# A two-layer hybrid encoder on one core: groups of the feed-forward part of 3, 4, 5, 5, 5 chunks instead of 4, 5, 5, 5, 3, and some weight lows by adding transfers

## The chip, the cores and the metric

The kernel runs on one core of a Trainium2 chip. The metric is the device time of one execution in microseconds (us). Engines are named as in the profile: PE (TensorE, matmul), PEld (its weight loads), DVE (VectorE), ACT (ScalarE), POOL (GpSimd), SP (SyncE, which issues the weight transfers). Each engine works through its own queue in the order in which the program was written; semaphores tie the queues together.

## The reference

Two layers over x of 512 tokens and 1024 features in float32. Each layer: an RMS norm; latents, queries, keys and values for two attentions, channels for a pooling branch, and gates; an attention with latent projections (MLA, 8 heads) and one with grouped queries (GQA, 8 heads on 2 key heads); the three branches projected, gated, summed, projected and added to x; then the feed-forward part, which this case is mostly about:

```python
D_MODEL, SEQ, DEPTH, D_FF = 1024, 512, 2, 2816

hf = rms_norm(x, ffn_norm_g[l])
u = depthwise_conv(hf @ ffn_w_up[l], ffn_conv_w[l], ffn_conv_b[l])   # width 3, along the tokens
u_gate, u_val = u[..., :D_FF], u[..., D_FF:]
x = x + (jax.nn.silu(u_gate) * u_val) @ ffn_w_down[l]
```

## The kernel before

**Numbers in two halves.** Features lie on the 128 partitions and the 512 tokens along the rows. Each float32 operand is split into a high half, rounded to the matmul's format, and a low half, the rest; a product is three matmuls, high by high, high by low, low by high (`mm3`). For activations the halves are `HH`, `HL` (the normed x) and `act` or `ah`, `al` (the gated product); for weights `wh`, `wl`, and `fh`, `fl` where a weight tile serves as an operand of its own.

**Weights.** SP's queue brings raw weight tiles in the order of use, into three wide tiles (`RAW`) and eight single ones (`ALONE`); a raw tile that comes free issues the next transfer. A unit of weights (128 x 512 or narrower) is split some units ahead of its use. The high is a copy on ACT. The low is made in one of two ways: a unit of kind "p" by a subtraction on DVE or POOL, whichever the planner thinks sooner; a unit of kind "u" by `by_transfer`: ACT writes the negative of the high, and a transfer that POOL issues adds the raw tile to it in memory.

```python
    def by_transfer(hi, lo, r):
        A.activation(hi, r, AF.Copy)
        A.activation(lo, f(hi), AF.Copy, scale=-1.0)
        ...
        nc.gpsimd.dma_start(f(lo), r, accum_op=ALU.add)
```

**What sets the order.** The program is written out by a planner while it records: a clock advances with each matmul, steps that depend on each other wait in chains (`chain`), and each is emitted to its engine's queue when the planner's estimate says that its time has come; `need` emits everything that an operand still lacks. The planner's costs only decide order; on the chip the engines wait for each other by semaphores.

**The stages of a layer.** Latents, pooling and GQA projections (0 to 82 us in the first layer); the two attentions, with projections, gates and branch outputs as fillers between their matmuls (to 355); the last of them and the output projection (to 427); the feed-forward part (to 772). The second layer does the same. In the attention, the scores' maxima use one PSUM bank, `ps_S`: a score matmul `ps_S<-ka,qa` writes it, a reduction `nm<-ps_S` on DVE reads it and frees it for the next. The "n" units are the key weights of the MLA attention, two units of 256 columns per layer.

**The feed-forward part.** The 2816 hidden features are 22 chunks of 128, each with a gate and a value part, in groups of `SIZES`. The first group is *plain*: each part is 24 matmuls of 512 columns (8 blocks of features by 3). The other chunks are *products*: four blocks of a 2 x 2 scheme are computed with seven half-size products instead of eight (`FORMS`, 84 matmuls of 256 columns per chunk), with sums of weight tiles (`s`, `raw<-raw,s`) and of activations (`tf`) as operands. Copies of banks between the products are the rows `sx<-ps_..` on ACT (`aside`): product "3" needs the copy that is made after product "2". The norm's factor `rbc` is applied when a bank is read; for the first plain parts `norm_finish` makes it: a small matmul `ps_S<-prt,C`, POOL's power, DVE's rows.

**The down-projection.** Each finished chunk gives `act`. Its *tokens* (g, m, i), three matmuls for output row m and chunk i of group g, are dealt into the products of the next group at four `SPOTS`; of the last but one group, two rows (`KEEP`) are kept for the end, where they are followed by the last group's own tokens. Output rows alternate between the banks mi and S; each is added to `XM` by DVE, which frees the bank. Places for `act` are kept by `keep_act`: six fixed ones for some chunks, slots of the common pool for others.

Of the kernel before, what the change touches and what calls it, by code (L numbers as in the profile page):

```python
# [41 lines left out]
PRE_A = 16  # L42
PRE_B = 8
LA, LAP, LAF = 3, 4, 6
SIZES = (4, 5, 5, 5, 3)
PLACE = (0, 4, 0, 5, 0)
ROOM = 6
KEEP = 2
FORMS = ("11", "12", "1", "22", "2", "4", "3")
SPOTS = ("22", "2", "4", "3")  # L50
# [4 lines left out]
        "mla": (-6.2, -2.9, -1.0, 0.1, 0.64, 1.678, 1.82, 35.5)}  # L55

D_ROW, D_OUT, D_IN, D_LAT = 3.4, 3.2, 4.0, 6.0
D_SUM, D_FIRST = 2.0, 2.4
D_ISSUE, D_ADD = 0.9, 4.5
REST = 0.4  # L60
W_BIAS = 2.54
# [14 lines left out]
def _order(br):  # L76

    r, lag = [], LAG[br]  # L80
    for m in range(KC + lag):
        r += [(k, pos.index(m)) for k, b, pos in EXTRA if b == br and m in pos]
        if m < KC:
            r.append(("g", m))
        if m >= lag:
            r.append(("b", m - lag))
    return r
# [6 lines left out]
def _widths():  # L94

    r = [384] * KC + [T] * 8 + [T] * KC + [288] * MID + [T] + [288] * (KC - MID)
    r = [("p", wd) for wd in r]
    for br in (2, 1, 0):
        late = []
        for k, m in _order(br):  # L100
            added = k in "gb" and br == 0 or br == 1 and (k == "v" or k == "g" and 1 <= m <= 3)
            ws = [("u" if added else "p", wd) for wd in WIDTHS[k]]
            if k in "nv":
                late = ws
            else:
                r += ws[:1] + late + ws[1:]
                late = []
    return r + [("u", T)] * (2 * KC)


def _groups():
    e = np.cumsum(SIZES)
    return [(int(b - n), int(b)) for n, b in zip(SIZES, e)]


def _ffn():
# [4 lines left out]
    for g, (c0, c1) in enumerate(_groups()):  # L121
        dealt = len(late) - (KEEP * SIZES[g - 1] if g == len(SIZES) - 1 else 0)
        for n, c in enumerate(range(c0, c1)):
# [14 lines left out]
def _layer_units():  # L138

    r = _widths()  # L140
    for tok in _ffn():
        if tok[0] == "u":
            r += [("u", T), ("p", T), ("next",)]
        elif tok[0] == "f":
            r.append(tok)
        elif (tok[2] * SIZES[tok[1]] + tok[3]) % 4 == 0:
            r.append(("u" if tok[1] < len(SIZES) - 1 else "p", T))
    return r


def _stream():


    pieces, slots, units, alone = [], [], [], []
    early, plain, fresh = [], 0, False
    for kind, *u in _layer_units() * L:
        if kind == "next":
            plain = (plain + 1) % (2 * SIZES[0])
            if plain and plain >= 2 * SIZES[0] - 8:
                early.append(len(slots))  # L160
                slots.append(T)
                alone.append(True)
            continue
        if kind == "f":
            if u[1] == FORMS[0]:
                first, fresh = len(pieces), True
                for _ in range(4):
                    if early:
                        pieces.append((early.pop(0), 0, T))
                        continue  # L170
                    pieces.append((len(slots), 0, T))
                    slots.append(T)
                    alone.append(True)
            units.append((u[1], first))
            continue
        if len(slots) <= KC or fresh or alone[-1] or slots[-1] + u[0] > 1024:
            slots.append(0)
            alone.append(False)
        fresh = False
        pieces.append((len(slots) - 1, slots[-1], u[0]))  # L180
        slots[-1] += u[0]
        units.append((kind, len(pieces) - 1))
    return pieces, slots, units, alone
# [25 lines left out]
class Clock:  # L209
# [37 lines left out]
    def done(self, *key):  # L247
        self.ready[key] = self.fin + self.SEM

    def need(self, *keys):  # L250
        for k in keys:
            while k not in self.ready:
                self.pop()
            self.to(self.ready[k])
# [4 lines left out]
    def chain(self, *steps, after=0.2):  # L259

        def go(n, source=None):
            if n == len(steps):
                return
            keys, fn = steps[n] if isinstance(steps[n], tuple) else ((), steps[n])
            late = [self.ready.get(k, self.now + 0.5) for k in keys]
            if late and max(late) > self.now:
                self.at(max(late) - self.now, lambda: go(n))
                return
            self.fin, self.source, self.last = self.now, source, None
            fn()  # L270
            source, self.source = self.last, None
            self.at(max(0.0, self.fin - self.now), lambda: go(n + 1, source))
        self.at(after, lambda: go(0))
# [65 lines left out]
def trunk(ctx: ExitStack, tc: tile.TileContext, x, w, prm, gb, cst, out):  # L339
    nc = tc.nc  # L340
    ctx.enter_context(tc.manual_schedule())
    ck = Clock()
# [16 lines left out]
    def slot(name, dt=F32):  # L359
        uid[0] += 1  # L360
        t = sp.tile([P, SLOT], dt, tag="s", name=f"{name}_{uid[0]}")
        return t
# [5 lines left out]
    def small(name, shape, dt=F32, bufs=2):  # L368
        uid[0] += 1
        t = sm.tile(shape, dt, tag=name, name=f"{name}_{uid[0]}", bufs=bufs)  # L370
        return t
# [4 lines left out]
    def ps(tag):  # L376
        while not banks[tag]:
            ck.pop()
        ck.to(heapq.heappop(banks[tag]))
        uid[0] += 1  # L380
        t = pp.tile([P, T], F32, tag=tag, name=f"ps_{tag}_{uid[0]}", bufs=nbank[tag])
        return t
# [8 lines left out]
    def free(tag):  # L391
        heapq.heappush(banks[tag], ck.fin + ck.SEM)
# [3 lines left out]


    pieces, swidth, units, alone = _stream()
    soff = np.concatenate([[0], np.cumsum(swidth)]) * P
    st = {"dma": 0, "split": 0, "use": 0, "ffn": False}  # L400
# [125 lines left out]
    def mm(o, lhsT, rhs, start, stop, again=False):  # L526
        PE.matmul(o, lhsT=lhsT, rhs=rhs, start=start, stop=stop, skip_group_check=again)  # L527
        n = rhs.shape[-1]
        ck.to(ck.now + (n / 2400.0 + 0.0133 if st["ffn"] else max(0.107, n / 2370.0)))
# [86 lines left out]

    def norm_finish(gen, out, force=False):

        if gen not in parts or not (force or ck.ready.get(("prt", gen), 1e9) + (D_FIRST if gen in (0, 1, 3) else D_SUM) <= ck.now):
            return  # L620
        need(("prt", gen))
        s2 = ps("S")
        mm(s2[:, :16], C[:, C_GRP:C_GRP + P], parts.pop(gen), True, True)
        a, a4 = small("fac", [P, 16]), small("fac4", [P, 16])
        rt, rbc = out["rt"], out["rbc"] = small("rt", [P, 4]), slot("rbc")

        def mean():
            V.tensor_scalar(a, s2[:, :16], 1.0 / D, EPS, ALU.mult, ALU.add)
            free("S")

        def tokens():
            V.tensor_tensor(a4, a, C[:, C_SEL:C_SEL + 16], ALU.mult)
            V.tensor_reduce(rt, a4.rearrange("p (b g) -> p b g", g=4), AX.X, ALU.add)
            done("rt", gen)

        def rows():
            V.transpose(rbc[:, :T].rearrange("p (j r) -> p j r", r=32), bc(a.unsqueeze(2), [P, 16, 32]))
            done("rbc", gen)

        chain(mean, lambda: G.tensor_tensor(a, a, bc(mhalf, [P, 16]), ALU.pow), tokens, rows, after=0.3)  # L640
# [13 lines left out]
    parts = {}  # L654

    def bc(ap, shape):
        return ap.to_broadcast(shape)
# [26 lines left out]
    def layer(l, sq, xsrc):  # L684
# [151 lines left out]
        for g in range(4):  # L836
            acc = ps(ptags[g])
            for n, _ in enumerate(feat_major(acc, G1)):
                norm_finish(G1, nrm, g == 1 and n == 7)
            chain(*pool_steps(g, acc, ptags[g]))  # L840
# [37 lines left out]
        for b in range(4):  # L878
            v = slot("vg", F32R)
# [769 lines left out]
        def keep_act(c):  # L1649
            g = next(i for i, (c0, c1) in enumerate(groups) if c0 <= c < c1)  # L1650
            i = c - groups[g][0]
            n = 2 * (PLACE[g] + i)
            if n < 2 * ROOM:
                return places[n], places[n + 1]
            return slot("ah", F32R)[:, :T], slot("al", F32R)[:, :T]

# [220 lines left out]
def _pack_weights(i):  # L1877
    res = []
    for l in range(L):
# [34 lines left out]
        for kind, *tok in _ffn():  # L1914
# [8 lines left out]
            elif kind == "d":  # L1923
                g, m, k = tok
                c0, c1 = _groups()[g]
                if (m * (c1 - c0) + k) % 4 == 0:
                    at = [divmod(m * (c1 - c0) + k + n, c1 - c0) for n in range(4)]
                    res.append(np.concatenate([dn[(c0 + k_) * P:(c0 + k_ + 1) * P, m_ * P:m_ * P + P]
                                               for m_, k_ in at], axis=1))
    pieces, swidth, _, _ = _stream()  # L1930
    assert [a.shape[1] for a in res] == [wd for _, _, wd in pieces]
    slots = [[] for _ in swidth]
# [79 lines left out]
```

## Time and profile before

| | |
|---|---|
| median of 3 runs | 1547.4 us (1546.53 to 1547.94) |
| profiled execution | 1548.79 us, span 1547.0 us |
| granted clock of TensorE | 1.000 |
| busy, share of the span | PE 99%, DVE 76%, ACT 69%, POOL 50% |
| transfers | 241.79 MB, 156 GB/s; queue q1 (SP) 34.3% of 16 engines, q0 (POOL) 29.0% |

The page gives busy times of each engine, the chain of work that ended last, groups of instructions and the time from a transfer's issue to its landing. The views quoted later are: the table by stage (for each stretch its length, and for each engine its busy time and number of instructions, then the granted clock, the transfers' share and GB/s), the waits of one engine (who was waited for, total, times, longest), the chain (start, length, what), and the timeline (start, length, engine, line, operation, output <- inputs, in brackets the idle time before it and who ended that). A matmul's row lasts longer than its share of TensorE, since matmuls are pipelined; the distance of two starts is what one costs.

### The profile page before, as it was taken

The page shows a single profiled execution, that of the slowest core. Times are in us where ns is not written, and L with a number is a line of the kernel's source. Part 1 is how long each engine was busy: PE and PEld are TensorE (multiplying, and loading weights), DVE is VectorE, ACT ScalarE, POOL GpSimd, SP SyncE. Part 2 cuts the span into 40 slices and gives each one's busy share as a digit, 9 for nine tenths or more (in the row PEclk, how much of TensorE's full clock was granted, in tenths as well). Part 3 has the DMA queues.
Part 4 walks back from the last instruction along what each step waited for, and adds up shares of the span by engine and source line. Part 5 has one row for each costly group of instructions (what it writes and reads, how often), then busy time and mean ns, then how long its engine had stood idle before and what let it go on. Part 6 is the DMA issues. An engine that isn't in the chain of part 4 may idle for free.

```text
span 1547.0 us, 24549 instructions
## 1 busy us (share of the span) xinstructions
PE 1537.7 (99%) x8337; PEld 1342.7 (87%) x8337; DVE 1169.6 (76%) x1960; ACT 1073.5 (69%) x2010; POOL 768.6 (50%) x826
## 2 busy tenths in 40 slices
PE   9999999999999999999999999999999999999998
PEld 8888888888889999999898888888888898999997
DVE  6877886776688888888656678768666888888884
ACT  5557875877677877777544587758766687777772
POOL 3984886753452323232488648766535422222222
PEclk9999999999999999999999999999999999999999
DMA  5432354658978788877534323546599778788763
GB/s 204 124 118 83 87 125 140 161 130 204 216 181 203 179 185 188 193 177 150 138 117 136 118 76 86 134 139 174 116 223 212 198 182 178 179 191 189 176 134 109
DMA packets 139517, 241.79 MB, mean 156 GB/s; under 512 B 30976, under 2 KB 53504, under 8 KB 139392
## 3 DMA queue, kind: packets, MB, share of 16 engines
q1 hardware_dynamic: 91872, 162.93, 34.3%
q0 software_dynamic: 42624, 77.09, 29.0%
q8 instruction: 65, 1.06, 0.3%
q10 hardware_dynamic: 4896, 0.21, 0.2%
q14 instruction: 60, 0.49, 0.1%
HBM read 149.41 MB, written 13.63 MB: 105 GB/s over the span
## 4 chain that ended last, share of the span: by engine, by line
PE 88%; issue 4%; DMA 3%; DVE 2%; POOL 2%; ACT 1%; SPq 0%; ACTq 0%; POOLq 0%; DVEq 0%
PE ps_acc L527 40%; PE ps_AV L527 16%; PE ps_ST L527 15%; PE ps_S L527 9%; PE ps_mi L527 8%; DMA raw<-w 1%; POOL wl L307 1%; DMA fl<-raw 1%; POOL win L307 0%; DMA wl<-raw 0%; DVE a L311 0%; ACT wh L300 0%; DMA qb<-nm 0%; DVE ctl L311 0%; DVE u L307 0%
## 5 line engine op out<-in xcount | busy, mean ns | idle before, releaser
L439 POOL DMA_DIRECT2D wl<-raw x188 | 168.9, 903 | 386.0 <-ACT wl L300 184.7
L300 ACT ACTIVATE wh<-raw 128x512 fp32r<-128x512 f32 (+2 forms) x449 | 265.1, 605 | 66.3 <-DVE raw L307 16.4
L307 POOL TENSOR_TENSOR wl<-raw,wh 128x512 fp32r<-128x512 f32 (+3 forms) x167 | 213.5, 1287 | 169.0 <-ACT wh L300 150.8
L439 POOL DMA_DIRECT2D fl<-raw x108 | 94.4, 874 | 168.6 <-ACT fl L300 62.7
L527 PE MATMUL ps_acc<-HH,wh 128*128 128x512 f32 x400 | 156.8, 392 | 0.4 <-DVE XM L311 0.4
L527 PE MATMUL ps_acc<-HH,wl 128*128 128x512 f32 x400 | 156.6, 391 | 0.1
L527 PE MATMUL ps_acc<-HL,wh 128*128 128x512 f32 x400 | 156.5, 391 | 0.0
L311 DVE SCALAR_TENSOR_TENSOR a<-u,prm,a 128x511 f32<-128x511 f32 x176 | 133.7, 762 | 22.8 <-ACT a L300 22.3
L300 ACT ACTIVATE wl<-wh 128x512 fp32r<-128x512 f32 (+1 forms) x188 | 118.1, 628 | 5.9
L315 DVE TENSOR_REDUCE nm<-ps_S 128x1 fp32r<-128x512 f32 x128 | 87.9, 687 | 44.8 <-PE ps_S L527 43.8
L300 ACT ACTIVATE a<-u,prm 128x512 f32<-128x512 f32 x88 | 71.2, 811 | 53.1 <-DVE u L307 52.9
L527 PE MATMUL ps_acc<-tf,wh 128*128 128x256 f32 x576 | 106.2, 282 | 0.0
L527 PEld LDWEIGHTS ps_acc<-tf,wh 128*128 128x128 f32 x576 | 94.3, 191 | 6.0
L527 PEld LDWEIGHTS ps_acc<-HH,wl 128*128 128x128 f32 x400 | 75.1, 188 | 16.7 <-DMA wl<-raw 0.5
L527 PEld LDWEIGHTS ps_acc<-HH,wh 128*128 128x128 f32 x400 | 75.4, 188 | 15.4 <-issue 0.7
L527 PEld LDWEIGHTS ps_acc<-HL,wh 128*128 128x128 f32 x400 | 75.3, 188 | 15.4
L307 DVE TENSOR_TENSOR wl<-raw,wh 128x512 fp32r<-128x512 f32 (+2 forms) x95 | 69.1, 728 | 20.0 <-ACT wh L300 19.5
L527 PE MATMUL ps_acc<-tf,wl 128*128 128x256 f32 x288 | 81.5, 283 | 0.0
L527 PE MATMUL ps_AV<-HH,wl 128*128 128x256 f32 (+1 forms) x240 | 78.2, 326 | 0.0
L527 PE MATMUL ps_AV<-HL,wh 128*128 128x256 f32 (+1 forms) x240 | 78.2, 326 | 0.0
L527 PE MATMUL ps_AV<-HH,wh 128*128 128x256 f32 (+1 forms) x240 | 78.2, 326 | 0.0
L300 ACT ACTIVATE fl<-fh 128x512 fp32r<-128x512 f32 x108 | 68.4, 633 | 3.4
(426 smaller groups left out, 5029.8 us busy)
## 6 DMA issues: line engine op xcount, KB each, us to landing
raw<-w SPq DMA_DIRECT2D x153, 512.0 KB, 4.0
wl<-raw POOLq DMA_DIRECT2D x184, 256.0 KB, 4.1
raw<-w SPq DMA_DIRECT2D x151, 256.0 KB, 3.7
fl<-raw POOLq DMA_DIRECT2D x108, 256.0 KB, 5.0
raw<-w SPq DMA_DIRECT2D x13, 384.0 KB, 3.1
XM<-x SPq DMA_DIRECT2D x16, 256.0 KB, 4.4
dtq<-tr SPq DMA_DIRECT2D x16, 192.0 KB, 2.0
dtk<-tr SPq DMA_DIRECT2D x16, 192.0 KB, 3.1
```

The costliest lines, as they stand in the source:

```text
L300: return self.eng.activation(out, in_, func, **k)
L307: return self.eng.tensor_tensor(out, *a)
L311: return self.eng.scalar_tensor_tensor(out, *a)
L315: return self.eng.tensor_reduce(out, in_, *a, **k)
L439: nc.gpsimd.dma_start(f(lo), r, accum_op=ALU.add)
L527: PE.matmul(o, lhsT=lhsT, rhs=rhs, start=start, stop=stop, skip_group_check=again)
```

## The change

- `SIZES` goes from 4, 5, 5, 5, 3 to 3, 4, 5, 5, 5: three plain chunks in place of four, and five chunks in the last group in place of three.
- `PLACE` names the places of `act` for each group: the first three chunks of every group get a fixed place, alternately 0 to 2 and 3 to 5, the others slots. `ROOM` is gone.
- The two "n" units of each layer become "u" units, whose lows are made by adding transfers.
- `_stream` gives early raw slots for single tiles after all six plain parts; before it did so after seven of eight.
- `D_FIRST` has one entry for each norm. Only the first differs: 3.2 in place of 2.4, the time after `prt` at which the planner emits the first norm's small matmul.

```diff
-SIZES = (4, 5, 5, 5, 3)
-PLACE = (0, 4, 0, 5, 0)
-ROOM = 6
+SIZES = (3, 4, 5, 5, 5)
+PLACE = ((0, 1, 2), (3, 4, 5), (0, 1, 2), (3, 4, 5), (0, 1, 2))
...
-D_SUM, D_FIRST = 2.0, 2.4
+D_SUM, D_FIRST = 2.0, (3.2, 2.4, 2.0, 2.4)
...
-            added = k in "gb" and br == 0 or br == 1 and (k == "v" or k == "g" and 1 <= m <= 3)
+            added = k in "gb" and br == 0 or br == 2 and k == "n" or br == 1 and (k == "v" or k == "g" and 1 <= m <= 3)
...
-            if plain and plain >= 2 * SIZES[0] - 8:
+            if plain >= 2 * SIZES[0] - 8 or not plain:
...
-        if gen not in parts or not (force or ck.ready.get(("prt", gen), 1e9) + (D_FIRST if gen in (0, 1, 3) else D_SUM) <= ck.now):
+        if gen not in parts or not (force or ck.ready.get(("prt", gen), 1e9) + D_FIRST[gen] <= ck.now):
...
-            n = 2 * (PLACE[g] + i)
-            if n < 2 * ROOM:
+            if i < len(PLACE[g]):
+                n = 2 * PLACE[g][i]
                 return places[n], places[n + 1]
```

The planner then writes another order in the attention and in the feed-forward part. Three places of it follow; names are the program's, and a number at a name's end only tells tiles apart.

DVE's queue in the first layer's attention (about 155 to 163 us of the profile), before:

```order
L311 SCALAR_TENSOR_TENSOR vt_1702<-ps_mi_1759,vg_73_587,vt_1702 128x512
L307 TENSOR_TENSOR wl_1817<-raw_1554,wh_1816 128x512
L327 RECIPROCAL oinv_1777<-otr_1776 128x16
L307 TENSOR_TENSOR wl_1845<-raw_1593,wh_1844 128x256
L307 TENSOR_TENSOR pl_1815<-ps_ST_1811,ph_1814 128x512
L315 TENSOR_REDUCE ssm_1028<-mns_1829 128x8
L315 TENSOR_REDUCE nm_1873<-ps_S_1874 128x1
L307 TENSOR_TENSOR gt_1885<-ps_acc_1793,rbc_404 128x512
L315 TENSOR_REDUCE ssm_1028<-mns_1864 128x8
L315 TENSOR_REDUCE nm_1873<-ps_S_1886 128x1
```

And of the changed program, from the same `vt` row:

```order
L310 SCALAR_TENSOR_TENSOR vt_1719<-ps_mi_1769,vg_73_581,vt_1719 128x512
L330 STREAM_TRANSPOSE otr_1789<-osum_1637 128x512
L326 RECIPROCAL oinv_1790<-otr_1789 128x16
L314 TENSOR_REDUCE ssm_1028<-mns_1825 128x8
L322 COPY MK_157<-ps_acc_1855 128x8x64
L306 TENSOR_TENSOR pl_1846<-ps_ST_1841,ph_1845 128x512
L306 TENSOR_TENSOR wl_1879<-raw_1598,wh_1878 128x512
L306 TENSOR_TENSOR gt_1876<-ps_acc_1791,rbc_409 128x512
L314 TENSOR_REDUCE ssm_1028<-mns_1863 128x8
L314 TENSOR_REDUCE nm_1894<-ps_S_1895 128x1
L310 SCALAR_TENSOR_TENSOR XM<-gt_1702,ps_acc_1877 128x512
```

Both weight lows (`wl`) ahead of the reduction `nm` are gone from DVE; a later unit's low stands there instead. POOL's queue in the changed program has them, the 256-wide one as a transfer (DMA) behind two subtractions:

```order
L306 TENSOR_TENSOR MQ_155<-MQ_155,ssm_1028 128x768
L306 TENSOR_TENSOR wl_1793<-raw_1559,wh_1792 128x512
L306 TENSOR_TENSOR MQ_155<-MQ_155,ssm_1028 128x768
L306 TENSOR_TENSOR wl_1810<-raw_1559,wh_1809 128x512
L438 DMA wl_1814<-raw_1598 128x256
```

ACT's queue at the first product chunk of the first layer (about 473 to 478 us), before, from the last plain part's convolution to the high of its `act`:

```order
L300 ACTIVATE a_5135<-u_5134,prm_91 128x512
L300 ACTIVATE sx_5138<-ps_acc_5140 128x256
L300 ACTIVATE wh_5161<-s_802_5112 128x512
L300 ACTIVATE wh_5186<-raw_4968 128x512
L300 ACTIVATE wl_5187<-wh_5186 128x512
L300 ACTIVATE fh_5208<-raw_4708 128x512
L300 ACTIVATE fl_5209<-fh_5208 128x512
L300 ACTIVATE sx_5139<-ps_AV_5185 128x256
L300 ACTIVATE act_4718<-a_5135 128x512
```

And after:

```order
L299 ACTIVATE a_5046<-u_5045,prm_91 128x512
L299 ACTIVATE wh_5072<-s_796_5023 128x512
L299 ACTIVATE wh_5095<-raw_4865 128x512
L299 ACTIVATE wl_5096<-wh_5095 128x512
L299 ACTIVATE fh_5120<-raw_4710 128x512
L299 ACTIVATE fl_5121<-fh_5120 128x512
L299 ACTIVATE sx_5050<-ps_AV_5094 128x256
L299 ACTIVATE fh_5140<-raw_4797 128x512
L299 ACTIVATE fl_5141<-fh_5140 128x512
L299 ACTIVATE sx_5050<-ps_ST_5119 128x256
L299 ACTIVATE act_4719<-a_5046 128x512
```

The pair `fh`, `fl` of the next weight tile and one more `sx` now stand ahead of the high of the last plain chunk's `act`.

ACT's queue in the last product chunk of the first layer (about 743 to 748 us), before; `sx_8480` is the copy that product "3" needs:

```order
L300 ACTIVATE sx_8481<-ps_ST_8543 128x256
L300 ACTIVATE wh_8577<-raw_8398 128x512
L300 ACTIVATE wl_8578<-wh_8577 128x512
L300 ACTIVATE sx_8480<-ps_acc_8482 128x256
L300 ACTIVATE wh_8607<-raw_8398 128x512
L300 ACTIVATE wh_8611<-raw_8584 128x512
L300 ACTIVATE a_8628<-u_8478,prm_91 128x512
```

And after, where it is `sx_8500`:

```order
L299 ACTIVATE sx_8501<-ps_ST_8561 128x256
L299 ACTIVATE wh_8587<-raw_8271 128x512
L299 ACTIVATE wl_8588<-wh_8587 128x512
L299 ACTIVATE wh_8592<-raw_8404 128x512
L299 ACTIVATE ah_8486<-a_8485 128x512
L299 ACTIVATE sx_8500<-ps_acc_8502 128x256
L299 ACTIVATE wh_8619<-raw_8404 128x512
L299 ACTIVATE wh_8645<-raw_8629 128x512
```

A weight copy (`wh_8592`) and the high of the chunk before (`ah_8486`) have come between.

## The prediction

> **What bounds the kernel now.** The page comes first: TensorE is busy for all but 9.3 us of the span, and 88% of the chain that ended last is matmul.
>
> ```profile
> span 1547.0 us, 24549 instructions
> PE 1537.7 (99%) x8337; PEld 1342.7 (87%) x8337; DVE 1169.6 (76%) x1960; ACT 1073.5 (69%) x2010; POOL 768.6 (50%) x826
> PE 88%; issue 4%; DMA 3%; DVE 2%; POOL 2%; ACT 1%; SPq 0%; ACTq 0%; POOLq 0%; DVEq 0%
> ```
>
> So time goes in two ways only: the matmuls that must be issued, and the few places where TensorE stands. The chain gives a matmul's price: 24 of 512 columns take 5.44 us (0.2267 each), 12 of 256 columns take 1.44 (0.120 each).
>
> ```profile
> 388.53 5.44 PE ps_ST L527 x24
> 473.70 1.44 PE ps_AV L527 x12
> ```
>
> The table by stage says where TensorE stands: almost nothing in the first layer's feed-forward part (355 to 704), but 0.75 us at its end, and 1.64 in one place of the second layer's.
>
> ```profile
> 355.00:470.00 115.00, 114.88 (x507) 94.47 (x507) 82.05 (x124) 77.25 (x137) 52.47 (x50) 1.00 0.89 212
> 470.00:704.00 234.00, 234.00 (x1641) 219.51 (x1640) 196.01 (x333) 179.35 (x334) 64.16 (x74) 1.00 0.82 184
> 704.00:760.00 56.00, 55.25 (x343) 49.54 (x342) 39.66 (x64) 35.49 (x66) 18.51 (x19) 1.00 0.60 130
> 1243.00:1300.00 57.00, 55.36 (x393) 51.95 (x392) 46.59 (x80) 43.34 (x82) 16.50 (x19) 1.00 0.85 191
> ```
>
> TensorE's own waits name them: one weight low that an adding transfer brought late, two waits for a PSUM bank at the end of a feed-forward part, two in the attention, one at the start.
>
> ```profile
> PE ps_ST L527 <- DMA fl<-raw: 1.6, 1, 1.6
> PE ps_S L527 <- DVE XM L307: 1.5, 2, 0.8
> PE ps_S L527 <- DVE nm L315: 0.6, 2, 0.3
> PE ps_S L527 <- DVE prt L315: 0.3, 1, 0.3
> ```
>
> All terms below are changes of the profiled execution, 1548.8 us (span 1547.0 and 1.8 around it); the median of the runs is 1547.4, and I carry the same difference over to it.
>
> **The matmul work: −1.5, certain.** In each layer one chunk goes from plain to seven half-size products. Plain it is 48 matmuls of 512 columns, 48 × 0.2267 = 10.88 us; as products 84 of 256, 84 × 0.120 = 10.08. That is −0.80 a layer, −1.60 in all. The last row of the output is done in halves over the last group, which grows from three chunks to five: its extra work is 12 more matmuls of 256 for 6 of 512, +0.08. Sum −1.52.
>
> **The lows of the "n" units by transfer: −1.7.** At 156 to 162 VectorE makes two weight lows itself and stands 1.29 us for ScalarE's high of the second. Behind it in the same queue are the reductions that free the score bank, S:
>
> ```profile
> 156.15 0.85 DVE L307 TENSOR_TENSOR wl<-raw,wh 128x512 fp32r<-128x512 f32 x1 [0.22 <-ACT wh L300]
> 158.45 1.53 DVE L307 TENSOR_TENSOR wl<-raw,wh 128x256 fp32r<-128x256 f32 x1 [1.29 <-ACT wh L300]
> 161.10 0.67 DVE L315 TENSOR_REDUCE nm<-ps_S 128x1 fp32r<-128x512 f32 x1
> 159.75 0.62 PE L527 MATMUL ps_S<-ka,qa 128*128 128x512 f32 x1
> 160.22 0.39 PE L527 MATMUL ps_AV<-ph,vg 128*128 128x512 f32 x1
> 161.14 0.40 PE L527 MATMUL ps_acc<-HH,wl 128*128 128x512 f32 x1
> 161.83 0.62 PE L527 MATMUL ps_S<-ka,qa 128*128 128x512 f32 x1 [0.29 <-DVE nm L315]
> 162.29 0.40 PE L527 MATMUL ps_ST<-qa,ka 128*128 128x512 f32 x1
> ```
>
> The starts of these matmuls should be 0.23 apart; they are 0.47, 0.69 and 0.46, so TensorE loses 0.24 + 0.46 + 0.23 = 0.93 a layer. In the new order both rows are gone from VectorE there: the 512-wide low is GpSimd's and the 256-wide one a transfer, and the two score matmuls stand further apart. I take 0.85 a layer. What speaks against it: the new transfer is issued only 7.3 us of matmuls before its use and stands behind two GpSimd subtractions. If those hold it for 2 us and it takes the page's median for such lows (4.1 us, below), 1.2 us are left. If it takes 8.12, as the slowest one quoted below, TensorE waits 2.8. Range −2.3 to +1.
>
> ```profile
> wl<-raw POOLq DMA_DIRECT2D x184, 256.0 KB, 4.1
> fl<-raw POOLq DMA_DIRECT2D x108, 256.0 KB, 5.0
> ```
>
> The Trainium skill ("SBUF — State Buffer", section "SBUF: two separate sides") has a rule against this edit: a transfer issued from GpSimd's queue waits while VectorE holds the ports the two share. By it the new low could be one VectorE row (0.7 us) later; 0.5 of the 1.2 would be left, and the sum stays. No row here shows such a wait by itself.
>
> **The start: −0.1.** The new first entry of `D_FIRST` puts the mean's matmul three matmuls later, which takes away the 0.3 wait for `prt` above. Its result is then 0.2 later for the chain of GpSimd steps that TensorE waits for at 76. Between −0.5 and +0.3.
>
> **The plain stage: −0.4.** Here transfers are the limit (share 0.89). One low landed 0.05 before its matmul, and 0.4 us of gaps lie around it:
>
> ```profile
> 453.89 6.15 DMA wl<-raw
> 460.09 5.30 PE ps_acc L527 x22
> ```
>
> One plain chunk fewer, and slots for the raw tiles of all six plain parts, give this stretch air. 0 to −0.5.
>
> **The first product chunk: +1.2.** What is new is a wait for the last plain chunk's activation. Now the product stage begins at 470.66, the low of that activation is done at 478.94, 8.28 later, and its first reader stands at 481.36:
>
> ```profile
> 470.66 0.28 PE L527 MATMUL ps_acc<-HH,fh 128*128 128x256 f32 x1
> 477.60 0.62 ACT L300 ACTIVATE act<-a 128x512 fp32r<-128x512 f32 x1
> 478.25 0.69 DVE L307 TENSOR_TENSOR act<-a,act 128x512 fp32r<-128x512 f32 x1 [1.00 <-ACT act L300]
> 481.36 0.63 PE L527 MATMUL ps_mi<-act,wh 128*128 128x512 f32 x2
> 443.00:471.00 28.00, 27.88 (x124) 22.71 (x123) 23.88 (x35) 20.30 (x33) 11.76 (x12) 1.00 0.87 211
> ```
>
> So 2.42 us are to spare. With three plain chunks the last one's first token is the third of the group instead of the fourth: the need moves three 512-wide matmuls and two products forward, to 8.56 (high) and 8.79 (low) after the start. The unchanged chain would leave 0.3 to 0.4. But in the new order two copies of feed-forward weights (`fh`, `fl`, 0.62 each) and one `sx` stand ahead of ScalarE's high, and VectorE, busy 24 of 28 us, has a weight low and a raw sum ahead of the scaling. I put the high at 7.9 to 8.6 and the low at 9.35: 0.6 late in each layer. From 0 (VectorE keeps its lead) to 1.5 a layer.
>
> **Short leads of adding transfers: −0.4.** One place costs 1.8 now: the low issued at 1291.05 took 8.12 us and its matmul, due at 1297.41, ran at 1299.21.
>
> ```profile
> 1291.05 8.12 DMA fl<-raw
> 1297.29 0.28 PE L527 MATMUL ps_ST<-HL,fh 128*128 128x256 f32 x1
> 1299.21 0.39 PE L527 MATMUL ps_ST<-HH,fl 128*128 128x256 f32 x1 [1.64 <-DMA fl<-raw]
> ```
>
> In the program this low is issued 6.8 us of matmuls ahead of its use, of which 6.4 were left on the chip. Counting so, the feed-forward part has three lows per layer now under 8 us: 6.8, 7.4 and 7.6. The new order keeps such a chunk (6.8, 7.6, 7.8) and adds thirteen more lows per layer: 7.0, 7.0, 7.3, twice 7.5, 7.5 and 7.6, and in the last group 7.7, 7.7, 7.8 and 8.0. A token of the down-projection is three 512-wide matmuls, 0.68 us, so a chunk with six tokens passes in 10.08 + 6 × 0.68 = 14.2 us; before, only the first product group (6.4 tokens) came near that. One of the six short ones is late now, by 1.8. For the 26 new ones, whose lead is 0.2 to 1.2 longer than that one's, I take half the chance and a third of the lateness: 26 / 12 × 0.6 = 1.3, and 0.1 for the old ones; 1.4 instead of 1.8. Range −1.8 (none late) to +5.
>
> The Trainium skill prices such a transfer at 2.0 us + bytes / 436e3 ("DMA: Bandwidth & Descriptors", section "Anatomy of one DMA — SWDGE (gpsimd) path"): 2.6 us for 256 KB, an estimate from that page. The trace disagrees: 5.0 at the median and 8.12 here. By the page no lead of 6.4 could be short, and this term would be −1.8; as a rival that is weighed below.
>
> **The end of each feed-forward part: −0.3.** TensorE now waits 0.75 for the S bank:
>
> ```profile
> 748.01 0.63 ACT L300 ACTIVATE wh<-raw 128x512 fp32r<-128x512 f32 x1 [2.19 <-PE ps_acc L527]
> 749.38 2.88 DVE L311 SCALAR_TENSOR_TENSOR a<-u,prm,a 128x511 f32<-128x511 f32 x2 [2.85 <-ACT a L300]
> 753.57 0.68 DVE L307 TENSOR_TENSOR XM<-ps_S,XM 128x512 f32<-128x512 f32 x1
> 754.31 0.74 PE L527 MATMUL ps_S<-act,wh 128*128 128x512 f32 x2 [0.75 <-DVE XM L307]
> 744.87 0.37 ACT L300 ACTIVATE sx<-ps_acc 128x256 f32<-128x256 f32 x1
> 746.50 0.40 PE L527 MATMUL ps_acc<-tf,wh 128*128 128x256 f32 x2
> ```
>
> ScalarE's weight copy held the convolution's first step, and VectorE's row that frees S stood behind the rest. With five chunks in the last group the bank is needed 0.6 us of matmuls later after more rows, and this stall (0.75 busy, 0.9 by starts) about goes: −1.0 a layer. But the last product ("3") needs the copy `sx` of the bank that product "2" wrote. Now that copy ends 1.27 before product "3". In the new order it stands behind a weight copy that waits for product "4" (2.8 after "2") and one more: 2.8 + 0.63 + 0.62 + 0.37 = 4.4 against 3.5 of matmuls, +0.85 a layer. Net −0.15 a layer, between −1.0 and +0.3.
>
> **Sum.** −1.5 −1.7 −0.1 −0.4 +1.2 −0.4 −0.3 = −3.2: 1545.6 for the profiled execution, 1544.2 for the median. That is just over what a measurement of this kernel can tell from no change, 0.2% or 3.1 us.
>
> **Rivals.**
> - *The waits eat the gain.* The activation is 1.5 us late in each layer (+3.0 for +1.2), and the score bank's wait only moves (−0.8 for −1.7): −0.5, 1546.9. For it: VectorE's 24 of 28 us. Against: the wait names the same bank in both layers, and its cause is gone from the queue.
> - *Slower: the six-token cadence makes lows late.* If a low in each of the five chunks with the shortest leads of a layer takes 8.1 as at 1291, they come 1.7, 1.5 and three times 1.0 late: 6.2 a layer, 12.4 in all in place of 1.8. With the other terms (−2.8) that is +7.8, 1555.2. It decides from 0.8 us a chunk on, ten chunks. For it: that one low, in the only group of such a cadence. Against: the same place of the first layer shows no wait, and one of 108 is late.
> - *Transfers and activation in time.* No low is late (−1.8), VectorE keeps its lead (0 for +1.2): −5.8, 1541.6. The page's rule above would give its first half.
>
> **How the numbers follow.** The forecast has 0.50; its own terms move it between −5 and −1, and a little over half of that lies beyond the bound: 0.29 faster, 0.21 same. Transfers and activation in time: 0.17, faster. The waits eat the gain: 0.21, same. Slower by late lows: 0.12. So faster 0.46, same 0.42, slower 0.12. The range, 1540.5 to 1549.0, takes in the first two rivals and small lateness, and leaves out the slow one and part of the best.
>
> **What would show it.** TensorE's busy time falls by about 1.5 to 2. VectorE's low of 256 columns is gone near 158, and the S score matmul there starts without a gap. At the third token of the first product group TensorE shows a wait for `act`, 0 to 1.5 us, in both layers; product "3" of the last chunk waits for `sx`, and XM's wait for S is gone. I am wrong if `fl` waits add up to more than 4 us, or if the attention's gaps are as long as before.

## The result, and the profile after

The changed kernel takes 1564.95 us (median of 4 runs, 1563.12 to 1566.65) against 1547.18 (median of 4, 1546.53 to 1547.94): 1.0116 times the time before, 95% interval 1.01 to 1.0132. It is 17.8 us slower; 1544.2 was forecast, and the range ended at 1549.0. The profiled execution took 1563.12 us, with a span of 1560.9 for 1547.0 before. Below, one execution of twice the usual length (the n units alone) and one of four times (the kernel before with seven buffers) are left out of the medians.

The page of the changed kernel (busy time, share and instructions of each engine; then the chain by engine) has the 78 more matmuls that the prediction counted, 8415 for 8337, and in the chain matmul has fallen from 88% to 86%, while VectorE and ScalarE have one more each:

```profile
PE 1541.8 (99%) x8415; PEld 1347.0 (86%) x8415; DVE 1172.6 (75%) x1971; ACT 1085.9 (70%) x2034; POOL 768.3 (49%) x825
PE 86%; issue 3%; DVE 3%; DMA 3%; POOL 2%; ACT 2%; SPq 0%; ACTq 0%; POOLq 0%; DVEq 0%
```

The waits of TensorE in the changed kernel (who was waited for; total, times, longest) name the place: not the feed-forward part, but the score bank S in the attention, twice 3.6 us.

```profile
PE ps_S L526 <- DVE nm L314: 7.2, 2, 3.6
PE ps_S L526 <- POOL qa L306: 2.0, 2, 1.0
PE ps_acc L526 <- ACT sx L299: 1.4, 2, 0.7
PE ps_ST L526 <- DVE gqr L306: 0.9, 1, 0.9
PE ps_ST L526 <- DMA fl<-raw: 0.5, 1, 0.5
```

The table by stage for the two attentions shows the size (length; PE busy and its matmuls first, granted clock behind the five engines). Before, then after, then the 20 us around the first wait, before and after:

```profile
82.00:355.00 273.00, 272.63 (x1220) 227.34 (x1219) 205.28 (x353) 197.90 (x371) 186.20 (x213) 1.00 0.45 119
850.00:1124.00 274.00, 273.28 (x1220) 227.36 (x1219) 206.21 (x354) 198.78 (x372) 184.77 (x211) 1.00 0.46 119
130.00:150.00 20.00, 20.00 (x93) 17.33 (x92) 15.80 (x30) 14.84 (x29) 9.48 (x13) 1.00 0.23 72
```

```profile
82.00:355.00 273.00, 268.06 (x1195) 223.21 (x1194) 200.65 (x341) 194.52 (x366) 184.34 (x212) 0.99 0.45 118
850.00:1124.00 274.00, 267.95 (x1203) 223.43 (x1202) 198.28 (x340) 195.74 (x366) 182.28 (x209) 0.99 0.45 117
130.00:150.00 20.00, 16.43 (x69) 13.80 (x67) 11.29 (x22) 11.72 (x23) 8.77 (x7) 0.91 0.25 72
```

In the same 20 us TensorE now issues 69 matmuls for 93, and the granted clock is 0.91. The timeline of that place, changed kernel: first ScalarE and VectorE, then TensorE.

```profile
134.28 0.63 ACT L299 ACTIVATE wh<-raw 128x512 fp32r<-128x512 f32 x1
139.21 0.42 ACT L299 ACTIVATE wh<-raw 128x256 fp32r<-128x256 f32 x1 [4.29 <-POOL wl L306]
139.98 0.51 ACT L299 ACTIVATE mqs<-MQ 128x384 f32<-128x384 f32 x1
140.96 0.59 ACT L299 ACTIVATE ps_mi<-ps_mi 128x512 f32<-128x512 f32 x1
140.52 0.55 DVE L314 TENSOR_REDUCE ssm<-mqs 128x4 f32<-128x384 f32 x1 [4.11 <-ACT mqs L299]
142.19 0.68 DVE L314 TENSOR_REDUCE nm<-ps_S 128x1 fp32r<-128x512 f32 x1
```

```profile
137.05 0.45 PE L526 MATMUL ps_S<-ka,qa 128*128 128x512 f32 x1
138.73 0.39 PE L526 MATMUL ps_acc<-HL,wh 128*128 128x512 f32 x1
138.96 0.39 PE L526 MATMUL ps_acc<-HH,wl 128*128 128x512 f32 x1
142.92 0.62 PE L526 MATMUL ps_S<-ka,qa 128*128 128x512 f32 x1 [3.58 <-DVE nm L314]
145.39 0.63 PE L526 MATMUL ps_AV<-ph,vg 128*128 128x512 f32 x1
145.81 0.63 PE L526 MATMUL ps_AV<-pl,vg 128*128 128x512 f32 x1
146.24 0.63 PE L526 MATMUL ps_AV<-vt,unit 128*128 128x512 f32 x1
```

The rows read as a chain. ScalarE stands 4.29 us for the high of a 256-wide weight: that is the *first* of the two n units. Its raw tile had landed at 128.7. It starts at 139.21, just after the matmul that started at 138.73 (`HL,wh`, to 139.12), the last reader of an older unit's high, is through; the last reader of that unit's low is the matmul at 138.96. Behind it in ScalarE's queue stand `mqs` and the exponential of the scores; behind those, on VectorE, `ssm`, and behind that the reduction `nm` that frees the score bank for the matmul at 142.92. TensorE loses 3.7 us by starts, and then issues matmuls 0.43 us apart instead of 0.23, which costs another 1.9. The second layer loses the same at its twin. Two later waits for `qa`, of 1.0 us each, follow near 200 and 974. The stops, the slow matmuls and these waits come to 13.6 us by starts, nearly all that the attentions grow by. The profile names POOL's `wl` as the releaser of ScalarE's row; it had ended 0.9 us before, and the runs below show what the row really waited for.

### The profile page after: what moved, and what is told of

It reads as the page before. It is cut to its first block, busy times and chain, and to the rows that moved or that the text cites. A ratio compares the mean times of both kernels' runs of the same rounds, so it can differ in the third digit from the quotient of the medians.

```text
span 1560.9 us, 24749 instructions
## 1 busy us (share of the span) xinstructions
PE 1541.8 (99%) x8415; PEld 1347.0 (86%) x8415; DVE 1172.6 (75%) x1971; ACT 1085.9 (70%) x2034; POOL 768.3 (49%) x825
## 4 chain that ended last, share of the span: by engine, by line
PE 86%; issue 3%; DVE 3%; DMA 3%; POOL 2%; ACT 2%; SPq 0%; ACTq 0%; POOLq 0%; DVEq 0%
PE ps_acc L526 38%; PE ps_AV L526 17%; PE ps_ST L526 15%; PE ps_S L526 8%; PE ps_mi L526 8%; DMA raw<-w 1%; POOL qa L306 1%; POOL wl L306 1%; DMA qb<-nm 0%; DMA fl<-raw 0%; ACT wh L299 0%; DVE nm L314 0%; DVE wl L306 0%; DMA qa<-nm 0%; SPq L860 0%
## 5 line engine op out<-in xcount | busy, mean ns | idle before, releaser
L438 POOL DMA_DIRECT2D wl<-raw x180 | 161.4, 900 | 374.1 <-ACT wl L299 243.4
L299 ACT ACTIVATE wh<-raw 128x512 fp32r<-128x512 f32 (+3 forms) x445 | 263.7, 606 | 81.3 <-DVE raw L306 15.7
L306 POOL TENSOR_TENSOR wl<-raw,wh 128x512 fp32r<-128x512 f32 (+2 forms) x168 | 214.7, 1286 | 152.9 <-ACT wh L299 146.0
L438 POOL DMA_DIRECT2D fl<-raw x114 | 100.2, 879 | 194.0 <-ACT fl L299 63.1
L526 PE MATMUL ps_acc<-HH,wh 128*128 128x512 f32 x384 | 150.4, 392 | 0.0
L526 PE MATMUL ps_acc<-HL,wh 128*128 128x512 f32 x384 | 150.1, 391 | 0.0
L526 PE MATMUL ps_acc<-HH,wl 128*128 128x512 f32 x384 | 150.0, 391 | 0.0
L299 ACT ACTIVATE wl<-wh 128x512 fp32r<-128x512 f32 (+1 forms) x180 | 112.3, 624 | 5.7
L526 PE MATMUL ps_acc<-tf,wh 128*128 128x256 f32 x608 | 112.2, 282 | 1.4 <-ACT sx L299 1.4
L306 DVE TENSOR_TENSOR wl<-raw,wh 128x512 fp32r<-128x512 f32 (+1 forms) x98 | 70.2, 717 | 15.5 <-ACT wh L299 14.6
```

Of the source, the lines that this page charges most:

```text
L299: return self.eng.activation(out, in_, func, **k)
L306: return self.eng.tensor_tensor(out, *a)
```

## The experiments

All ratios are against runs of the kernel before on the same chip, whose median was 1547.2 to 1547.7 in the four batches.

**Which part of the change.** The first batch splits it. The n units put back to subtraction in the changed kernel:

```diff
-added = k in "gb" and br == 0 or br == 2 and k == "n" or br == 1 and ...
+added = k in "gb" and br == 0 or br == 1 and ...
```

> The changed kernel with the two "n" units of each layer put back to subtraction; groups, places, early slots and D_FIRST stay. Theory A (the loss comes from the first n unit: its high stands on ScalarE's queue 4.3 us for a weight buffer and holds the rows that free the score bank, once per layer): the stalls at 139 and 913 are gone, the attention's gaps are those of before (5.5 and 6.3 us), and the time is 1545 to 1547.5. Theory B (the loss is made in the feed-forward part or by the transfers as a whole): it stays above 1558. Theory C (half and half): 1552 to 1557.

Measured 1551.36 (9 runs, 1547.66 to 1552.98), ratio 1.002 (1.0009 to 1.0031): 13.6 us come back. The waits of 3.6 us are gone. The time is 3.9 us over the expected range; in the profiled execution a wait for `act`, of which more below, is 2.0 us of that; the rest is spread over smaller waits.

The reverse, the kernel before with the n units alone:

> The kernel before with only the two n units by adding transfer. Theory A: TensorE waits 3.6 us for nm at the same score matmul in both layers and runs slowly just behind it, 14 to 18 us in all: 1561 to 1565. Theory B: as before or a little faster, 1545 to 1548. Theory C: 1552 to 1557.

Measured 1560.92, 13.3 us slower, ratio 1.0086 (1.007 to 1.0101), and TensorE's waits (this kernel) show the same two:

```profile
PE ps_S L527 <- DVE nm L315: 7.2, 2, 3.6
PE ps_S L527 <- POOL qa L307: 1.7, 2, 1.0
```

The groups, places and early slots alone:

> The groups, places and early slots alone, on the kernel before (D_FIRST 2.4 for the first norm, n units by subtraction): what the feed-forward part is worth. By the trace of the changed kernel: matmul work -1.5, gaps of the feed-forward parts +0.8 and -1.0: 1545 to 1546.5. By the prediction's sum (-1.5 -0.4 +1.2 -0.4 -0.3): 1545.8. Against the run without n transfers it shows D_FIRST: the trace of the changed kernel has 1.2 us more gaps in the first 82 us, so it should be 0.5 to 1.2 faster than that; by the prediction's term 0.1 slower.

Measured 1548.46 (11 runs, 1547.36 to 1552.35), ratio 1.001 (1.0001 to 1.0018): slower by some 1 us, not faster by 1.6. And `D_FIRST` alone:

> The kernel before with the new first entry of D_FIRST alone. The prediction's term: -0.5 to +0.3. The two runs with and without it (groups with and without D_FIRST) differ by 2.9 in the median, their traces by 1.0 in the first 82 us (wait for gqr 0.9). If that 1.0 is all of it: 1548.2 to 1549.2, the rest of the 2.9 being scatter between runs; if D_FIRST also shifts what follows: 1550 to 1551.

Measured 1548.43, ratio 1.0006 (0.9998 to 1.0015): not told apart from nothing, but its trace has the new 0.9 us wait for `gqr`, and the gaps of the first 82 us add up to 4.9 us against 3.9. The 2.9 us between the two runs with groups are therefore not all D_FIRST's.

**Early, or a transfer?** The first n unit is not only a transfer now; as a unit of kind "u" it also makes the look-ahead four units instead of three. Its high then stands 40 matmuls earlier in the program, which is 8.7 us by their starts in the trace before (132.74 to 141.41); the 5.5 us of the expectation below is too little. Here the n units stay transfers and the look-ahead stays three:

```diff
-ws = [("u" if added else "p", wd) for wd in WIDTHS[k]]
+ws = [(("t" if k == "n" else "u") if added else "p", wd) for wd in WIDTHS[k]]
```

("t" is split like "u" and counted like "p" in the look-ahead.)

> The changed kernel whose n units stay transfers, but count as plain units in the look-ahead, so that they are split three units ahead of their use instead of four; the first one's high is then written 5.5 us of matmuls later. If the early high alone is the cause (theory A): no wait of 3 us at the score bank, 1544 to 1548, and the second n unit shows whether the transfer gains the 0.9 per layer that the prediction gave it (then 1 to 2 us under the run without n transfers). If the transfer itself is the cause (its issue, its landing, its ports): above 1556.

Measured 1552.14, ratio 1.0033 (1.002 to 1.0046): 12.8 us come back with the transfers still there. The waits of 3.6 us are gone, so the early high is the cause, not the transfer. In this kernel's ScalarE timeline the first n unit's high (256 wide) runs 9 us after the high before it; in the changed kernel it stood directly behind that one, at 134.28.

```profile
134.82 0.63 ACT L299 ACTIVATE wh<-raw 128x512 fp32r<-128x512 f32 x1
143.98 0.41 ACT L299 ACTIVATE wh<-raw 128x256 fp32r<-128x256 f32 x1
```

The expected time was missed by some 4 us, about as much as without n units. In this kernel's attention, smaller waits come in place of the old gaps near 161.

```profile
PE ps_S L526 <- DVE nm L314: 1.3, 2, 0.7
PE ps_ST L526 <- DVE vt L310: 1.1, 2, 0.6
```

**What the high waits for.** Weight halves live in six pairs of buffers. This is the changed kernel with seven; each engine has the same instructions in the same order.

```diff
-NSLOT = 47
+NSLOT = 45
-hlp = ctx.enter_context(tc.tile_pool(name="hlp", bufs=LA + 3))
+hlp = ctx.enter_context(tc.tile_pool(name="hlp", bufs=LA + 4))
```

> The changed kernel, each engine's instructions in the same order word for word, with seven pairs of weight buffers instead of six (and 45 common slots instead of 47, to pay for them). Theory A (the first n unit's high waits for a weight buffer that TensorE still reads): ScalarE does not stand at 135 to 139, the waits of 3.6 us for nm are gone in both layers, and about 12 of the 17 us come back: 1549 to 1554. Rival A2 (it waits for its raw tile, or the order itself is bad): the 3.6 us waits stay, 1562 to 1566. Rival A3 (two slots fewer cost as much elsewhere): the nm waits go, but others come; the run of the kernel before with the same buffers tells it.

Measured 1558.83, ratio 1.0077 (1.0065 to 1.0089). At the place itself the wait is gone: this kernel's ScalarE writes both highs at 134.09 without a stop, and the score matmul follows the one before it by 0.24.

```profile
134.09 0.94 ACT L299 ACTIVATE wh<-raw 128x512 fp32r<-128x512 f32 x2
135.38 0.51 ACT L299 ACTIVATE mqs<-MQ 128x384 f32<-128x384 f32 x1
138.91 0.40 PE L526 MATMUL ps_acc<-HH,wl 128*128 128x512 f32 x1
139.15 0.40 PE L526 MATMUL ps_S<-ka,qa 128*128 128x512 f32 x1
```

So the high waited for a weight buffer. Only 6.1 of the 17.8 us come back, though: a wait of 2.8 us for `nm` stands at 170 and at its twin of the second layer instead, and the waits for `qa` stay. The control, the kernel before with seven buffers and 45 slots, has such waits for `nm` too, of 2.0 us:

> The kernel before with seven weight buffers and 45 slots, the control for the two runs above. Buffers alone matter little, since no long wait of it is for one: 1546 to 1548.5. If two slots fewer cost, it is slower than 1549.

Measured 1552.58, ratio 1.0035 (1.0022 to 1.0048), with 5.0 us of waits for `nm` where the kernel before has 0.6. Its order is the old one, so the exchange itself costs 5.4 us, most likely by the two slots (no run has 45 slots and six buffers), and is no repair. That is about half of the 11.6 us by which the run above stays slower. For the rest its trace has, by starts and beyond the control's, 4.3 us more of gaps in the attentions and some 4 us of waits for `act`, and 1.6 us less of matmul work. The same exchange on the groups:

> Groups, places and early slots on the kernel before, with seven weight buffers and 45 slots. If product 3's wait for sx (0.86 us at the end of each feed-forward part) has the same cause, a weight's high that waits for its buffer ahead of sx on ScalarE, it goes: 1546 to 1547.5 against 1548.5 with six buffers, perhaps under the kernel before. If it stays or slots are missed: 1548 to 1552.

Measured 1554.76, ratio 1.0048 (1.0036 to 1.006). The wait for `sx` did go (no row of it is left), so it has the same cause. The time is lost in the attention as in the control, and in waits for `act` (3.9 us by starts).

**The two n units apart.** On the kernel before, the first of each layer only:

```diff
-added = k in "gb" and br == 0 or br == 1 and ...
+added = k in "gb" and br == 0 or br == 2 and k == "n" and m == 0 or br == 1 and ...
```

> The kernel before with only the first n unit of each layer by adding transfer. Theory A (the early high of this unit is the whole loss): nearly all of the 13.6 us of both units, 1558 to 1562, with the wait of 3.6 us for nm at 139 and its twin, and slow matmuls behind it. If the second unit does half of it: 1552 to 1556.

Measured 1565.49, ratio 1.0114 (1.0099 to 1.013): 18.0 us, the whole loss and more than both units together (13.3). Beside the waits of 3.6 us there are longer ones for `qa`, which stands on GpSimd's queue:

```profile
PE ps_S L527 <- DVE nm L315: 7.5, 4, 3.6
PE ps_S L527 <- POOL qa L307: 4.0, 2, 2.1
```

And the second only (`m == 1`):

> The kernel before with only the second n unit of each layer by adding transfer; this is the low on which the prediction's -1.7 rests. By that term: the gaps of 0.93 at the score matmuls near 161 go and the time is 1545 to 1546.5. By the run in which both units were transfers with a look-ahead of three (gaps at 161 gone, new ones at 168 and 217 of 1.1 and 0.7): 1548 to 1551.

Measured 1545.74 (10 runs, 1544.46 to 1547.43), ratio 0.9989 (0.998 to 0.9998): 1.8 us faster. The gaps that the prediction read are closed as it said, in this kernel's TensorE timeline 0.24 and 0.25 where there were 0.69 and 0.46; only the first distance, 0.46, stays.

```profile
160.10 0.62 PE L527 MATMUL ps_S<-ka,qa 128*128 128x512 f32 x1
160.56 0.39 PE L527 MATMUL ps_AV<-ph,vg 128*128 128x512 f32 x1
161.48 0.40 PE L527 MATMUL ps_acc<-HH,wl 128*128 128x512 f32 x1
161.72 0.42 PE L527 MATMUL ps_S<-ka,qa 128*128 128x512 f32 x1
161.97 0.39 PE L527 MATMUL ps_ST<-qa,ka 128*128 128x512 f32 x1
```

Last, the changed kernel with the first unit alone put back:

> The changed kernel with one thing put back: the first n unit of each layer by subtraction, the second stays a transfer. If the first unit is the whole loss of the n units: the sum of the parts, groups +0.8 to 1.2, D_FIRST +0.9, second unit -1.8: 1546.5 to 1549.5, with the score bank's waits of 3.6 us gone. If the loss needs both: above 1555.

Measured 1548.15 (12 runs), ratio 1.0003 (0.9995 to 1.0012): one of the change's edits, on one unit of each layer, makes 16.8 of the 17.8 us.

**Where the saved matmul work goes.** The groups alone should save 1.5 us and save nothing. Two repairs were tried on them. In the last product chunk two products split weights four units ahead instead of six, so that a weight copy fewer stands ahead of `sx`:

```diff
-            wh, wl = wnext()
+            wh, wl = wnext(4 if c == FC - 1 and name in ("22", "2") else LAF)
```

> The same with the first repair alone. The wait for sx is 1.4 in all on the groups' trace (1.7 by starts): 1546.5 to 1547.5 against 1548.5 without it. If the copy only makes another row late: 1548 to 1549.

Measured 1551.06 (9 runs, 1547.45 to 1554.4), ratio 1.0022 (1.0012 to 1.0031). No wait for `sx` is left, but the wait for VectorE's `XM` at the end of the feed-forward part is back, up to 1.9 us. It only moves; this trace also has the wait for `act`, 1.2 us in the second layer.

The other repair gives the tokens of the second group two later, so that the last plain chunk's `act` is needed 1.44 us later:

```diff
-now = late[:dealt * (n + 1) // (c1 - c0) - dealt * n // (c1 - c0)]
+share = [dealt * i // (c1 - c0) - 2 * (g == 1 and 0 < i < c1 - c0) for i in range(c1 - c0 + 1)]
+now = late[:share[n + 1] - share[n]]
```

> The groups, places and early slots (no n units, no D_FIRST) with the second repair alone: the first four chunks of the second group get their tokens two later, so that the third token, which needs the last plain chunk's act, comes 1.44 us later. If the wait for act is what scatters the runs with groups (1547.4 to 1552.4): no wait for act, 1546.5 to 1548 and a spread under 2.5 us. If the spread comes from transfers in general: 1548 to 1550 with a spread of 4 or more.

Measured 1547.34 (11 runs, 1546.08 to 1550.61), ratio 1.0 (0.9991 to 1.0008). The wait for `act` is gone from this kernel's waits; the median is 1.1 us under the groups alone (in another batch, and the intervals overlap). The spread is 4.5 us instead of 5.0, so the wait for `act` is not what scatters the runs; the kernel before itself spreads over 3.1 to 4.9 us in the four batches. Both repairs together:

> The groups without the n units and without D_FIRST, with two repairs: in the last product chunk products 22 and 2 split weights four units ahead instead of six, so that one weight copy fewer stands ahead of the sx that product 3 needs; and the first four chunks of the second group get two tokens fewer each way up to them, so that the third token, which needs the last plain chunk's act, comes 1.44 us later. If the waits for sx (0.86 a layer) and act (up to 2 a layer in some runs) are what eats the 1.5 us of matmul work: 1545 to 1546.5, under the kernel before (1547.2 to 1547.7). If they only move: 1547.5 to 1549.

Measured 1547.4, ratio 1.0002 (0.9994 to 1.0011): no gain over the second alone. In the same batch it is 3.7 us under the first repair alone, and the intervals do not overlap, so the wait for `act` is part of what the groups lose.

**A version under both kernels.** The groups with the later tokens, and the second n unit:

> The same with the second n unit of each layer by adding transfer, the first by subtraction. If the parts add (-1.8 for the second unit as measured alone): 1545 to 1546.5, under both kernels. If not: 1547 to 1549.

Measured 1546.11 (12 runs, 1544.11 to 1548.91), ratio 0.999 (0.9982 to 0.9999). It beats both kernels, by 1.3 us the one before, and so does the second n unit alone (1545.74). The two are not told apart; the groups add nothing that these runs can show.

## Why the prediction was wrong

- **Matmul work, −1.5: right.** 78 more matmuls, as counted; with each matmul priced at the median distance of its shape over all 17 traces, the sum falls from 1522.3 to 1520.7 us.
- **The lows of the n units, −1.7: the step that failed.** It was argued on the unit whose wait the trace showed, the second, and for that unit it holds: −1.8 alone. The other unit was not walked through at all. It had no wait before, so nothing in the trace pointed at it; but the edit changes its kind, the kind sets the look-ahead, and the look-ahead puts its high 8.7 us of matmuls earlier on ScalarE's queue, ahead of rows that free the score bank and at a time when all six weight buffers are in use. As measured the term is +13.3 on the kernel before and +13.6 in the changed one, in place of −1.7; the bounds "−2.3 to +1" priced only how late the new transfer could land. The sentence that the wait "names the same bank in both layers, and its cause is gone from the queue" was true and beside the point. In the trace of the changed kernel the gaps of the two attentions, counted against the same median distances, grow by 6.7 and 7.6 us, 14.3 in all; the span grows by 13.9. The prediction had named this sign of being wrong itself: gaps in the attention as long as before.
- **The start, −0.1: wrong in sign, small.** `rbc` 0.2 later was thought to be within the wait that follows; the wait for `gqr` became 0.9 where 0.3 was. In the runs it is not told from nothing.
- **The plain stage, −0.4: right by luck.** The gaps there are gone in the changed kernel, but none of the five other traces with the old groups has them in the first layer's plain stage either. The 0.4 belonged to the one execution that was profiled, so no run shows that the groups remove it.
- **The first product chunk, +1.2: the mechanism was right, the size varies.** The need did move forward to 8.57 us after the start of the product stage, where 8.56 was worked out (by three 512-wide matmuls and one product; the prediction says two products). The third token waits for `act`, 0.4 us a layer by starts in the changed kernel's trace and in that of the groups alone; in the kernel without n units 2.0 in the second layer (rows below). In every trace with the new groups it is about 0.4 or about 2.0, and none in the three with the token later.

```profile
1237.76 0.39 PE L526 MATMUL ps_mi<-act,wl 128*128 128x512 f32 x1
1239.45 0.49 PE L526 MATMUL ps_mi<-act,wh 128*128 128x512 f32 x1 [1.30 <-ACT act L299]
1240.18 0.50 PE L526 MATMUL ps_mi<-act,wh 128*128 128x512 f32 x1 [0.23 <-DVE act L306]
```

- **Short leads, −0.4: near by luck.** The wait of 1.64 us at 1299 is gone, and one of 0.5 us appears at another low. But the five other traces with the old groups have 0 to 0.7 us of such waits, and those with the new groups 0 to 1.7. The 1.6 that the term saved on was one execution's, and no run shows its sign. The rival without any late low falls too: late lows stay in most of the traces. The slow rival, late lows throughout, did not come either: in no trace do the waits for them add up to more than 1.7 us.
- **The end of the feed-forward part, −0.3: the mechanism was right.** Product 3 waits for `sx`, 0.86 by starts in both layers, where 0.85 was worked out, and the wait for `XM` all but goes. What is left of the two comes to about zero instead of −0.15 a layer:

```profile
743.24 0.63 ACT L299 ACTIVATE wh<-raw 128x512 fp32r<-128x512 f32 x1 [1.52 <-PE ps_AV L526]
744.29 0.36 ACT L299 ACTIVATE sx<-ps_acc 128x256 f32<-128x256 f32 x1
744.71 0.51 PE L526 MATMUL ps_acc<-tf,wh 128*128 128x256 f32 x2 [0.70 <-ACT sx L299]
```

The same mechanism, a weight's high that waits for its buffer and holds what stands behind it, was thus read and priced here within 0.01 us, and not looked for at the first n unit.

What stays open: why the first n unit alone costs more than both (18.0 against 13.3; its `qa` waits are twice as long), why the kernel without n units is 2.9 us slower than the groups alone, and what scatters the runs by 3 to 5 us, those of the kernel before too.

## What to carry to other kernels

When an edit changes the class of several instructions, walk through every member and not only the one with the visible wait: ask for each where it moves in its queue, what its destination still holds there, and what is queued behind it. In an in-order queue, work that is emitted earlier is not free: a write whose buffer is still being read stops everything behind it, and a longer look-ahead that needs a buffer still in use turns into a wait. And the profile's releaser can be the wrong one; one more buffer with an unchanged order told here what the row had waited for.

## What the runs showed of the hardware

A stop of TensorE costs more than its length. After the wait of 3.58 us the distance of 512-column matmuls is 0.43 us instead of 0.23 for about 3 us (rows above), 0.91 of the clock over those 20 us. The Trainium skill ("TensorE: Matmul & The Clock Gate", section "What's actually happening") says that the array's clock is halved after an idle window of about 3.4 us and released after a busy one; the halved rate and its length agree. But shorter stops did it here as well: the kernel with the first n unit alone shows it after a wait of 1.90,

```profile
197.66 0.62 PE L527 MATMUL ps_S<-ka,qa 128*128 128x512 f32 x1 [1.90 <-POOL qa L307]
198.48 0.63 PE L527 MATMUL ps_AV<-pl,vg 128*128 128x512 f32 x1
198.90 0.63 PE L527 MATMUL ps_acc<-HH,wh 128*128 128x512 f32 x1
199.33 0.63 PE L527 MATMUL ps_acc<-HL,wh 128*128 128x512 f32 x1
```

while before, after the wait of 1.64 at 1299, the next matmuls come at 0.22 and then 0.12. Over all 17 traces, counted by the distance of starts beyond the usual: the eight stops of 3.0 to 3.7 us are all followed by the half rate, three of the seven of 2.0 to 2.2 us, and none of the 26 of 1.0 to 1.8. In two of the kernels a stop of 2.2 us at the same place was followed by it in the second layer and not in the first. Where the half rate followed, the slow matmuls cost about 2 to 3 us on top of the stop.
